# The gate projection's second half as one of SSD's concurrent streams

## The chip, the cores and the metric

The kernel runs on one core of one Trainium2 chip. The metric is the time of one execution in device microseconds (us). Before the change the median of three runs is 3372.4 us (3372.23 to 3380.13). The engines are TensorE (PE in rows; PEld its weight loads), VectorE (DVE), ScalarE (ACT), GpSimd (POOL) and SyncE (SP), which here only issues DMAs. Each engine works through its own list in a fixed order.

## The reference

The model is two transformer-like blocks on 1024 tokens of width 1024. The change lies in the first block's token mixers: a gated delta rule (GDN, 4 heads of 128) and a Mamba-2 SSD (8 heads of 64), each in both directions, both gated by a projection z of the same normalised tokens, and joined by an output projection.

```python
proj = h @ w_in
q, k, v, z_g, a_g, b_g, z_s, x_s, B_s, C_s, dt_s = _split(proj, GDN_SPLITS + SSM_SPLITS)
...
o = o_f + _flip(o_b)
o = rmsnorm(o, gdn_norm_g) * jax.nn.silu(z_g.reshape(Bsz, L, GDN_HEADS, GDN_DV).astype(f32))
...
y = y_f + _flip(y_b) + ssm_D.astype(f32)[:, None] * xs.astype(f32)
y = rmsnorm(y.reshape(Bsz, L, SSM_W) * jax.nn.silu(z_s.astype(f32)), ssm_norm_g)
mix = jnp.concatenate([o, y.astype(f32)], axis=-1).astype(h.dtype)
```

Only z_g (512 columns) and z_s (512 columns), their silu, and what multiplies them matter here. The output projection then multiplies mix by w_out, and the rest of the model follows.

## The kernel before

The kernel is written with a tile framework. Its program is emitted in an order of phases (phase_a, phase_gdn, phase_ssd, phase_mix, then the feed-forward part and the second block), and a list scheduler makes from it, ahead of time, one fixed list of instructions per engine; what is emitted earlier has priority, and a ready instruction of a later phase may be placed into a gap. Tiles come from pools with a number of buffers, so an instruction that takes a buffer waits for the last reader of the one it replaces.

phase_a projects the tokens and writes what later phases need to DRAM: the normalised tokens hxd (8 chunks of 128 tokens, each with a high and a low part, 1 MB a chunk), x (xtd), C (CTd), B (btd, BTd), k and v (ktd, vtd). Float32 products of the large projections are made of three matmuls in a reduced form, high by high, high by low, low by high.

phase_gdn works on 10 chunks (two of context) in two directions: a preparation (prep) for each of 20 chunk and direction pairs builds and inverts a triangular system on TensorE, VectorE and ScalarE in turns (Z products L580, D from a broadcast load, L496, in three buffers), and a step per pair carries the state and adds its output into oacc (L668). At its end the function zunits (L710) emits the gate projection zz: four quarters of 256 columns, each of which reads all 8 token chunks again (32 loads hx of 1 MB, L719, issued by GpSimd), 24 matmuls of 128x256 for a chunk (L722, 768 in all), a silu on 128x512 for two chunks (L725) and a write of the block to DRAM (zd, L726). It has one PSUM bank (psZ). It is emitted behind GDN, so the scheduler places it in gaps of GDN and among SSD.

phase_ssd (L728) drives several generators in turns: two chains of steps (L806 xe, L810 po, L826 pst), two of diagonal parts (diag: D0 and D1 masks and exps, xs, pcb, py L788), gdn_out (squares of oacc, L851, then the normalised and gated GDN output, L863) and ssd_out (product of yacc and the gate, L879, square L881, scaling L886, then chunk(): transposes ptm L909 and copies into the tile mixt). Each step and each diag loads its x, C and B from DRAM. mixt shares two on-chip slots (hx 2 and 3) with the gate's weights and tokens, so it waits for the last zz. phase_mix (L955) begins with the output projection pw (L980).

Of the kernel before, what the change touches and what calls it, by code (L numbers as in the profile page):

```python
# [23 lines left out]
def layout(inp):  # L24
    f = {k: np.asarray(v) for k, v in inp.items()}
    o = {}
# [25 lines left out]
    o["wz"] = np.ascontiguousarray(np.concatenate([zg, zs], 1).reshape(8, 128, 4, 256).transpose(2, 1, 0, 3))  # L52
# [68 lines left out]
class K:  # L121
# [63 lines left out]
    def phase_a(self):  # L185
# [136 lines left out]
        self.gcol = pp.tile([128, 1], F32, name="gcol")  # L322
        nc.gpsimd.dma_start(self.gcol, bass.AP(tensor=T["hp"].tensor, offset=T["hp"].offset + 56, ap=[[1, 128], [1, 1]]))
# [180 lines left out]
    def phase_gdn(self):  # L504
# [5 lines left out]
        psz = self.pool("psZ", 1, PSUM, ctx=zx)  # L510
# [21 lines left out]
        def prep(c, d, sl):  # L532
# [7 lines left out]
            D = ld.tile([128, 4, 128], F32, name="D")  # L540
# [76 lines left out]
        def step(c, d):  # L617
# [84 lines left out]
        self.zunits(psz, zp)  # L702
# [3 lines left out]
    def zunits(self, psz, zp):  # L706
        nc, T = self.nc, self.T
        HX = self.hx(3, [128, 2, 2, 8, 128], F32R)
        WZ = self.hx(2, [128, 2, 8, 256], F32R)
        for q in range(4):  # L710
            for k in range(0, 8, 2):
                raw = zp.tile([128, 2, 256], F32, name="raw")
                nc.sync.dma_start(raw, T["wz"][q][:, k:k + 2, :])
                self.split(WZ[:, 0, k:k + 2, :], WZ[:, 1, k:k + 2, :], raw)
            for c0 in range(0, 8, 2):
                zz = psz.tile([128, 2, 256], F32, name="zz")
                for i in range(2):
                    hx = HX[:, i]
                    nc.gpsimd.dma_start(hx, self.hxd[c0 + i])  # L719
                    for k in range(8):  # L720
                        for j, (a, b) in enumerate(((0, 0), (0, 1), (1, 0))):
                            nc.tensor.matmul(zz[:, i, :], hx[:, a, k, :], WZ[:, b, k, :],  # L722
                                             start=k == 0 and j == 0, stop=k == 7 and j == 2)
                zs = zp.tile([128, 2, 256], F32, name="zs")
                nc.scalar.activation(zs, zz, AF.Silu)  # L725
                nc.scalar.dma_start(self.zd[c0:c0 + 2, :, 256 * q:256 * q + 256].rearrange("c p f -> p c f"), zs)  # L726

    def phase_ssd(self):  # L728
# [7 lines left out]
        self.mixt = [[self.hx(i, [128, 8, 512], F32R) for i in (2, 3)]]  # L736
        self.psx = ExitStack()
# [11 lines left out]
        def loads(c, tag):  # L749
            x = ld.tile([128, 8, 64], F32, name="xt", tag="xt" + tag)  # L750
            nc.sync.dma_start(x.rearrange("p h f -> p (h f)"), self.xtd[c])
            ct = None
            if c < 8:
                ct = ld.tile([128, 2, 128], F32, name="CT", tag="CT" + tag)
                nc.sync.dma_start(ct, self.CTd[:, :, c * 128:(c + 1) * 128].rearrange("g p t -> p g t"))
            return x, ct

        def diag(c):
            x, ct = loads(c, "d")
            BT = ld.tile([128, 2, 128], F32, name="BT")  # L760
            nc.sync.dma_start(BT, self.BTd[:, :, c * 128:(c + 1) * 128].rearrange("g p t -> p g t"))
            xd = pr.tile([128, 8, 64], F32, name="xd")
            nc.gpsimd.tensor_tensor(xd, x, self.hp[:, 48:56, None].to_broadcast([128, 8, 64]), op=ALU.mult)
            D, X = [], []
# [78 lines left out]
        def gdn_out():  # L843
            ss = fp.tile([128, 8, 4], F32, name="ss")
            rs = fp.tile([128, 8, 4], F32, name="rs")
            for _ in range(6):
                yield
            for c in range(8):
                for h in range(4):
                    sq = fp.tile([128, 128], F32, name="sq", bufs=2)  # L850
                    nc.scalar.activation(sq, self.oacc[:, c, h, :], AF.Square, accum_out=ss[:, c, h:h + 1])  # L851
                yield
# [15 lines left out]
        def ssd_out():  # L868
            for i in range(4):
# [3 lines left out]
                while min(done[c] for c in cs) < 3:  # L873
                    yield
# [1349 lines left out]
```

## Time and profile before

| | us |
|---|---|
| median of three runs | 3372.4 |
| profiled execution | 3373.24 |
| its span in the trace | 3371.1 |
| TensorE busy in the span | 3088.8 |
| VectorE | 1841.7 |
| ScalarE | 1171.6 |
| GpSimd | 509.0 |

All times of the trace are from the start of the span. A stretch's busy time is what the engine's instructions fill. The granted clock is TensorE's, as a share of 2.4 GHz. An idle stretch of an engine counts only where the others wait for it. The rows that the prediction rests on stand below, each in a group with its view.

### The profile page before, as it was taken

What the parts mean: (1) busy time and instruction counts of PE and PEld (TensorE: products, weight loads), DVE (VectorE), ACT (ScalarE), POOL (GpSimd) and SP (SyncE); (2) the same over time, 40 slices, a digit from 0 to 9 for tenths busy, and PEclk for the clock granted to TensorE, in tenths of its full rate; (3) what the DMA queues carried; (4) which work ended last, traced back from release to release, by engine and by line L of the source; (5) the groups of instructions that cost most, each with busy time, mean ns of one, the idle gap of its engine ahead of it and who ended that gap; (6) DMA issues with size and microseconds to landing.
All of it is one profiled execution on the core that took longest, in us unless ns stands there. A gap on an engine that the chain in (4) does not pass through costs nothing. (4 is left out here: it accounts for less than half of the span.)

```text
span 3371.1 us, 43138 instructions
## 1 busy us (share of the span) xinstructions
PE 3088.8 (92%) x16679; PEld 2327.3 (69%) x16679; DVE 1841.7 (55%) x3344; ACT 1171.6 (35%) x2568; POOL 509.0 (15%) x416
## 2 busy tenths in 40 slices
PE   7999799877999999999999899999999997988886
PEld 3788689776788888888787787777777784322222
DVE  5754589557666564564778822458886454100000
ACT  4432455544432221122445512237775221111110
POOL 0000355344300000000233200000000101111110
PEclk9999799988999999999999999999999997999999
DMA  6942432786211111111211122200004458999996
GB/s 223 292 133 67 143 127 92 234 288 234 81 58 57 47 50 48 44 50 50 75 51 42 40 75 94 70 32 25 26 14 148 171 189 341 399 399 392 400 396 259
DMA packets 178188, 502.12 MB, mean 149 GB/s; under 512 B 21391, under 2 KB 85519, under 8 KB 148287
## 3 DMA queue, kind: packets, MB, share of 16 engines
q1 hardware_dynamic: 134928, 413.88, 33.5%
q0 software_dynamic: 14832, 52.81, 5.0%
q10 hardware_dynamic: 28223, 32.67, 2.7%
q8 instruction: 132, 2.16, 0.3%
q14 instruction: 73, 0.60, 0.1%
HBM read 450.39 MB, written 67.23 MB: 154 GB/s over the span
## 5 line engine op out<-in xcount | busy, mean ns | idle before, releaser
L2071 PE MATMUL ph<-wraw,xTt 128*64 128x512 f32 x1056 | 283.5, 606 | 49.1 <-DMA wraw<-in_w_dram 45.6
L158 ACT CAST wh<-wf 128x1024 fp32r<-128x1024 f32 x128 | 134.1, 1049 | 531.8 <-PE pg L943 187.2
L941 PE MATMUL pg<-hx,wh 128*128 128x512 f32 (+1 forms) x864 | 263.5, 385 | 8.5 <-DVE xt L1289 6.4
L943 PE MATMUL pg<-hx,wh 128*128 128x512 f32 (+1 forms) x864 | 262.4, 384 | 0.0
L945 PE MATMUL pg<-hx,wl 128*128 128x512 f32 (+1 forms) x864 | 262.1, 384 | 0.0
L2071 PEld LDWEIGHTS ph<-wraw,xTt 128*64 128x64 f32 x1056 | 84.5, 138 | 222.1 <-issue 122.6
L1069 DVE SCALAR_TENSOR_TENSOR acc<-pad,fcw,acc 128x1024 f32<-128x1024 f32 x176 | 226.0, 1284 | 21.3 <-ACT acc L1066 16.8
L159 DVE TENSOR_TENSOR wl<-wf,wh 128x1024 fp32r<-128x1024 f32 x96 | 117.0, 1219 | 136.2 <-ACT wh L158 135.6
L941 PEld LDWEIGHTS pg<-hx,wh 128*128 128x128 f32 x864 | 161.7, 190 | 41.5 <-ACT ainh L158 6.8
L943 PEld LDWEIGHTS pg<-hx,wh 128*128 128x128 f32 x864 | 161.7, 190 | 32.0
L945 PEld LDWEIGHTS pg<-hx,wl 128*128 128x128 f32 x864 | 161.5, 190 | 32.1 <-DVE wl L159 0.3
L722 PE MATMUL zz<-hx 128*128 128x256 f32 x768 | 131.7, 314 | 37.7 <-DMA hx<-hxd 21.0
L2088 PE MATMUL py<-wraw,hT 128*64 128x512 f32 x528 | 150.2, 601 | 3.7 <-issue 2.8
L2074 DVE SCALAR_TENSOR_TENSOR hs<-ph,gate,hs 128x256 f32<-128x256 f32 x32 | 15.5, 484 | 250.7 <-ACT hs L2073 250.7
L722 PEld LDWEIGHTS zz<-hx 128*128 128x128 f32 x768 | 109.2, 207 | 44.4 <-DMA hx<-hxd 15.4
L1027 POOL TENSOR_TENSOR sx<-sx,sqx 128x1024 f32<-128x1024 f32 x7 | 20.2, 2880 | 723.8 <-ACT sqx L1026 723.8
L1105 DVE SCALAR_TENSOR_TENSOR x<-pd,mod,x 128x1024 f32<-128x1024 f32 x42 | 53.9, 1282 | 136.3 <-PE pd L1100 136.3
L2092 DVE COPY yt<-py 128x512 f32<-128x512 f32 x33 | 22.8, 692 | 187.2 <-ACT yt L2091 187.2
L2073 ACT ACTIVATE hs<-ph 128x256 f32<-128x256 f32 x33 | 12.6, 383 | 282.0 <-PE ph L2071 282.0
L159 POOL TENSOR_TENSOR wl<-wf,wh 128x1024 fp32r<-128x1024 f32 x32 | 84.1, 2631 | 138.9 <-ACT wh L158 138.9
L225 PE MATMUL pj<-hxh,wh 128*128 128x512 f32 x320 | 103.4, 400 | 0.0
L225 PE MATMUL pj<-hxl,wh 128*128 128x512 f32 x320 | 102.6, 399 | 0.0
(702 smaller groups left out, 7565.6 us busy)
## 6 DMA issues: line engine op xcount, KB each, us to landing
wraw<-in_w_dram SPq DMA_DIRECT2D x132, 1024.0 KB, 22.3
wraw<-in_w2e_dram SPq DMA_DIRECT2D x66, 1024.0 KB, 22.9
hx<-hxd POOLq DMA_DIRECT2D x32, 1024.0 KB, 7.0
wa<-in_wadaT_dram SPq DMA_DIRECT2D x32, 512.0 KB, 5.0
wf<-in_wgate_dram SPq DMA_DIRECT2D x22, 512.0 KB, 3.2
wf<-in_wup_dram SPq DMA_DIRECT2D x22, 512.0 KB, 3.2
wf<-in_wconv_dram SPq DMA_DIRECT2D x20, 512.0 KB, 3.2
wdf<-in_wdown_dram SPq DMA_DIRECT2D x40, 256.0 KB, 2.6
```

Of the source, the lines that this page charges most:

```text
L158: nc.scalar.copy(hi, x)
L159: (eng or nc.vector).tensor_tensor(lo, x, hi.bitcast(F32), op=ALU.subtract)
L225: nc.tensor.matmul(ps[:, o:o + n], w[:, k, :], (hl if lo else hh)[:, k, ho:ho + n], start=k == 0 and i == 0, stop=k == 7 and i == 2)
L722: nc.tensor.matmul(zz[:, i, :], hx[:, a, k, :], WZ[:, b, k, :], start=k == 0 and j == 0, stop=k == 7 and j == 2)
L941: nc.tensor.matmul(ps[:, o:o + n], wh[:, k, :], xh[:, k, o:o + n], start=k == 0, stop=False)
L943: nc.tensor.matmul(ps[:, o:o + n], wh[:, k, :], xl[:, k, o:o + n], start=False, stop=False)
L945: self.lastmm = nc.tensor.matmul(ps[:, o:o + n], wl[:, k, :], xh[:, k, o:o + n], start=False, stop=k == nk - 1)
L1069: nc.vector.scalar_tensor_tensor(acc, pad[:, dy:dy + 16, dx:dx + 64], cw[:, f, tp:tp + 1], acc, op0=ALU.mult, op1=ALU.add)
L1105: nc.vector.scalar_tensor_tensor(x, pp, self.mod2[:, 24 + m:25 + m], x, op0=ALU.mult, op1=ALU.add)
L2071: nc.tensor.matmul(ph[m], x[:, k, m], f[s][:, j, :], start=k == 0, stop=k == 7)
L2088: nc.tensor.matmul(py[m, o * 512:o * 512 + 512], h[:, j, m], f[s][:, 2 * j + o, :], start=j == 0, stop=j == 1)
L2092: nc.vector.tensor_copy(y[:, 512:1024], py[:, 512:1024])
```

## The change

The weights are laid out as two halves of 512 columns, GDN's gate and SSD's gate. The function zunits goes away. The first half is emitted at the end of phase_gdn: all its weights are split once into two slots (hx 2, 3) from 16 raw loads of 128x256 through one buffer; tokens come in pieces of 256 KB (two of the eight 128-row blocks, high and low) into one tile hxs with room for two pieces, 4 loads a chunk, 32 in all; 24 matmuls of 128x512 a chunk; the silu is done in two halves of 256 columns through one buffer zs, each followed by a write.

The second half is a generator zgen in SSD's drive: four weight loads of 512 KB, split into the same two slots; per chunk (in the order 3, 4, 2, 5, 1, 6, 0, 7) two token loads of 512 KB into buffers that the output projection's weights also use (wpW), 24 matmuls, one silu, one write. ssd_out waits for zgen's chunk, and mixt is taken only when zgen is done. psZ's one bank stays through SSD, and SSD's own PSUM banks go from 6 to 5. In SSD x (10 tiles), C (one 1 MB load) and B by rows (one load) are loaded once and kept on chip; BT keeps a load per chunk. In GDN D has two buffers instead of three, and the squares of oacc move from gdn_out into the step that finishes a chunk.

```diff
-    o["wz"] = np.ascontiguousarray(np.concatenate([zg, zs], 1).reshape(8, 128, 4, 256).transpose(2, 1, 0, 3))
+    o["wz"] = np.ascontiguousarray(np.concatenate([zg, zs], 1).reshape(8, 128, 2, 512).transpose(2, 1, 0, 3))
...
-            D = ld.tile([128, 4, 128], F32, name="D")
+            D = ld.tile([128, 4, 128], F32, name="D", bufs=2)
...
+            nc.vector.tensor_add(oc, t, po2)
+            if c in seen:
+                for h in range(4):
+                    nc.scalar.activation(t[:, h, :], oc[:, h, :], AF.Square, accum_out=self.ssg[:, c, h:h + 1])
             seen.add(c)
-            nc.vector.tensor_add(oc, t, po2)
...
-        self.zunits(psz, zp)
+        self.zw = [self.hx(i, [128, 8, 512], F32R) for i in (2, 3)]
+        for k in range(16):
+            raw = zp.tile([128, 256], F32, name="raw")
+            f = (slice(None), k // 2, slice(256 * (k % 2), 256 * (k % 2) + 256))
+            nc.sync.dma_start(raw, T["wz"][0][f])
+            self.split(self.zw[0][f], self.zw[1][f], raw)
+        hx = zp.tile([128, 2, 4, 128], F32R, name="hxs")
+        for c in range(8):
+            zz = psz.tile([128, 512], F32, name="zz")
+            for k in range(0, 8, 2):
+                nc.gpsimd.dma_start(hx[:, :, k % 4:k % 4 + 2, :], self.hxd[c, :, :, k:k + 2, :])
+                for k2 in (k, k + 1):
+                    self.zmm(zz, hx[:, 0, k2 % 4, :], hx[:, 1, k2 % 4, :], k2)
+            for o in (0, 256):
+                zs = zp.tile([128, 256], F32, name="zs")
+                nc.scalar.activation(zs, zz[:, o:o + 256], AF.Silu)
+                nc.scalar.dma_start(self.zd[c, :, o:o + 256], zs)
         st.close()
         zx.close()
 
-    def zunits(self, psz, zp):
-        nc, T = self.nc, self.T
-        HX = self.hx(3, [128, 2, 2, 8, 128], F32R)
-        WZ = self.hx(2, [128, 2, 8, 256], F32R)
-        for q in range(4):
-            for k in range(0, 8, 2):
-                raw = zp.tile([128, 2, 256], F32, name="raw")
-                nc.sync.dma_start(raw, T["wz"][q][:, k:k + 2, :])
-                self.split(WZ[:, 0, k:k + 2, :], WZ[:, 1, k:k + 2, :], raw)
-            for c0 in range(0, 8, 2):
-                zz = psz.tile([128, 2, 256], F32, name="zz")
-                for i in range(2):
-                    hx = HX[:, i]
-                    nc.gpsimd.dma_start(hx, self.hxd[c0 + i])
-                    for k in range(8):
-                        for j, (a, b) in enumerate(((0, 0), (0, 1), (1, 0))):
-                            nc.tensor.matmul(zz[:, i, :], hx[:, a, k, :], WZ[:, b, k, :],
-                                             start=k == 0 and j == 0, stop=k == 7 and j == 2)
-                zs = zp.tile([128, 2, 256], F32, name="zs")
-                nc.scalar.activation(zs, zz, AF.Silu)
-                nc.scalar.dma_start(self.zd[c0:c0 + 2, :, 256 * q:256 * q + 256].rearrange("c p f -> p c f"), zs)
+    def zmm(self, zz, h, l, k):
+        for j, (a, b) in enumerate(((h, 0), (h, 1), (l, 0))):
+            self.nc.tensor.matmul(zz, a, self.zw[b][:, k, :], start=k == 0 and j == 0, stop=k == 7 and j == 2)
...
-        ps = self.pool("psS", 6, PSUM, ctx=st)
+        ps = self.pool("psS", 5, PSUM, ctx=st)
         pr = self.pool("sprep", 3, ctx=st)
-        ld = self.pool("sld", 3, ctx=st)
+        ld = self.pool("sld", 1, ctx=st)
...
+        X = [ld.tile([128, 8, 64], F32, name=f"X{c}") for c in range(10)]
+        CT = ld.tile([128, 2, 1024], F32, name="CT")
+        bts = ld.tile([128, 10, 256], F32, name="bts")
+
+        def load(c):
+            nc.sync.dma_start(X[c].rearrange("p h f -> p (h f)"), self.xtd[c])
+
+        for c in (8, 9):
+            load(c)
+        nc.sync.dma_start(bts, self.btd.rearrange("c p f -> p c f"))
+        nc.sync.dma_start(CT, self.CTd.rearrange("g p t -> p g t"))
+        for c in (0, 1, 7, 2, 6, 3, 5, 4):
+            load(c)
...
-                while min(done[c] for c in cs) < 3:
+                while min(done[c] for c in cs) < 3 or not zc.issuperset(cs):
...
-                    while gdone[0] < 2 * i + 2:
+                    while gdone[0] < 2 * i + 2 or not zdone:
                         yield
                     yield
+                    if not self.mixt:
+                        self.mixt.append([self.hx(i, [128, 8, 512], F32R) for i in (2, 3)])
                     for c in cs:
                         self.chunk(c)
                         yield
 
-        self.drive([chain(0), chain(1), diags(0), diags(1), gdn_out(), ssd_out()])
+        zc, zdone = set(), []
+
+        def zgen():
+            for k in range(0, 8, 2):
+                raw = self.wpW.tile([128, 8, 128], F32, name="wf").rearrange("p (a b) c -> p a (b c)", a=2)
+                nc.sync.dma_start(raw, T["wz"][1][:, k:k + 2, :])
+                self.split(self.zw[0][:, k:k + 2, :], self.zw[1][:, k:k + 2, :], raw)
+            yield
+            for c in (3, 4, 2, 5, 1, 6, 0, 7):
+                zz = self.psz.tile([128, 512], F32, name="zz")
+                hl = [self.wpW.tile([128, 8, 128], F32R, name=n) for n in ("wh", "wl")]
+                for j in range(2):
+                    nc.gpsimd.dma_start(hl[j], self.hxd[c, :, j])
+                for k in range(8):
+                    self.zmm(zz, hl[0][:, k, :], hl[1][:, k, :], k)
+                    if k % 4 == 3:
+                        yield
+                zs = fp.tile([128, 512], F32, name="zs")
+                nc.scalar.activation(zs, zz, AF.Silu)
+                nc.scalar.dma_start(self.zd[c, :, 512:1024], zs)
+                zc.add(c)
+            zdone.append(1)
+
+        self.drive([chain(0), chain(1), diags(0), diags(1), zgen(), gdn_out(), ssd_out()])
```

The lists of the engines before and after are the same from the first pw matmul on. Ahead of it these places differ.

TensorE, from the last po of GDN (from vo and P) into SSD's first matmuls, before (zz is the gate projection, pcb, pst, po and py are SSD's):

```order
4862 L663 MATMUL po_7273<-vo,P 128x128 x4
4863 L722 MATMUL zz<-hx 128x256 x37
4864 L775 MATMUL pcb<-CT,BT 128x128 x2
4865 L722 MATMUL zz<-hx 128x256 x48
4866 L775 MATMUL pcb<-CT,BT 128x128 x2
4867 L826 MATMUL pst<-xe,bt 128x256 x4
4868 L722 MATMUL zz<-hx 128x256 x48
4869 L826 MATMUL pst<-xe,bt 128x256
4870 L722 MATMUL zz<-hx 128x256 x24
4871 L826 MATMUL pst<-xe,bt 128x256 x3
4872 L810 MATMUL po<-hT_8250,CT 128x256
4873 L722 MATMUL zz<-hx 128x256 x6
```

The same place after:

```order
4793 L729 MATMUL zz<-hx,hxs 128x512
4794 L665 MATMUL po_7302<-vo,P 128x128 x4
4795 L729 MATMUL zz<-hx,hxs 128x512 x26
4796 L785 MATMUL pcb<-CT,BT 128x128 x4
4797 L835 MATMUL pst<-xe,bts 128x256
4798 L729 MATMUL zz<-hx,hxs 128x512 x12
4799 L835 MATMUL pst<-xe,bts 128x256 x4
4800 L729 MATMUL zz<-hx,hxs 128x512 x6
4801 L835 MATMUL pst<-xe,bts 128x256
4802 L729 MATMUL zz<-hx,hxs 128x512 x6
4803 L835 MATMUL pst<-xe,bts 128x256 x2
4804 L819 MATMUL po<-hT_7697,CT 128x256 x2
```

Before, 217 of 768 zz stand ahead of GDN's last solve (pn) and 264 ahead of the first pcb; after, 19 and 50 of 384.

TensorE, from SSD's last matmuls to the first pw, before:

```order
5057 L788 MATMUL py<-xs_8941,D_8934 128x64
5058 L826 MATMUL pst<-xe,bt 128x256 x4
5059 L810 MATMUL po<-hT_8250,CT 128x256 x2
5060 L810 MATMUL po<-hT_8251,CT 128x256 x2
5061 L909 MATMUL ptm<-cst,hx 128x128 x32
5062 L980 MATMUL pw<-hx,wh 128x512 x3
5063 L980 MATMUL pw<-hx,wl 128x512
```

After (the zz from wh and wl tiles are zgen's; what is left out between the pieces is zz alone, with two ptm):

```order
4980 L798 MATMUL py<-xs_8448,D_8441 128x64
4981 L819 MATMUL po<-hT_7698,CT 128x256 x2
4982 L729 MATMUL zz<-hx,wh 128x512 x2
4983 L729 MATMUL zz<-hx,wl 128x512
...
5061 L729 MATMUL zz<-hx,wl 128x512
5062 L938 MATMUL ptm<-cst,hx 128x128 x6
5063 L729 MATMUL zz<-hx,wh 128x512 x2
...
5111 L729 MATMUL zz<-hx,wl 128x512
5112 L938 MATMUL ptm<-cst,hx 128x128 x24
5113 L1009 MATMUL pw<-hx,wh 128x512 x3
5114 L1009 MATMUL pw<-hx,wl 128x512
```

All 192 zz of zgen stand behind SSD's last po, and 8 of the 32 transposes ptm stand between them; before there is no zz behind SSD's last zz groups, and the 32 ptm follow po at once.

ScalarE, at the end of SSD's exps (L502 in before, L503 after), before:

```order
480 L725 ACT_TABLE_LOAD
481 L725 ACTIVATE zs<-zz 128x512
482 L502 ACT_TABLE_LOAD
483 L502 ACTIVATE D_8891<-D_8891,fneg 128x128
484 L726 DMA zd<-zs 128x2x256
485 L881 ACTIVATE sqy,sy<-hx 128x512
486 L502 ACTIVATE D_8934<-D_8934,fneg 128x128 x8
487 L725 ACT_TABLE_LOAD
488 L725 ACTIVATE zs<-zz 128x512
489 L881 ACTIVATE sqy,sy<-hx 128x512
490 L726 DMA zd<-zs 128x2x256
```

After (zs of L722 are the two halves of a block, CAST of wf is zgen's weights):

```order
487 L722 ACT_TABLE_LOAD
488 L722 ACTIVATE zs<-zz 128x256
489 L503 ACT_TABLE_LOAD
490 L503 ACTIVATE D_8441<-D_8441,fneg 128x128
491 L723 DMA zd<-zs 128x256
492 L503 ACTIVATE D_8441<-D_8441,fneg 128x128 x2
493 L722 ACT_TABLE_LOAD
494 L722 ACTIVATE zs<-zz 128x256
495 L723 DMA zd<-zs 128x256
496 L722 ACTIVATE zs<-zz 128x256
497 L723 DMA zd<-zs 128x256
498 L158 CAST hx<-wf 128x1024 x4
499 L919 ACTIVATE zs<-zz 128x512
```

Each block of a chunk now has two silus with a write between them, and exps and their table load stand between the halves; the casts of zgen's weights stand behind the last half. In all 27 table loads stand in SSD's part of the list, 18 before.

## Rows read from the trace of the kernel before

**Rows 1.** Head of the page.
```profile
span 3371.1 us, 43138 instructions
```

**Rows 2.** Timeline, TensorE and VectorE: start us, us, engine, line, operation, count [idle].
```profile
628.71 0.69 DVE L668 TENSOR_TENSOR hx<-ot,po 128x512 f32<-128x512 f32 x1 [4.26 <-POOL ot L666]
...
804.87 2.08 PE L810 MATMUL po<-hT,CT 128*128 128x256 f32 x8 [2.21 <-DVE hT L832]
...
829.40 1.94 PE L909 MATMUL ptm<-cst,hx 128*128 128x128 f32 x8 [4.02 <-DVE hx L886]
...
832.66 1.20 PE L980 MATMUL pw<-hx,wh 128*128 128x512 f32 x2
```

**Rows 3.** Stretches: length, busy us (instructions) by engine, clock, DMA share, GB/s.
```profile
400.00:628.00 228.00, 216.06 (x2937) 207.33 (x2934) 193.22 (x506) 125.30 (x368) 110.09 (x125) 0.98 0.34 109
...
640.00:800.00 160.00, 129.66 (x881) 120.56 (x880) 82.95 (x107) 79.18 (x191) 74.51 (x74) 0.91 0.85 283
...
820.00:840.00 20.00, 12.97 (x45) 9.61 (x44) 18.03 (x63) 4.57 (x8) 0.00 (x0) 0.54 0.80 288
```

**Rows 4.** Waits, 640 to 840: who waited for what, us, times, longest.
```profile
POOL hx L719 <- PE zz L722: 46.2, 11, 9.1
...
PE zz L722 <- DMA hx<-hxd: 17.8, 7, 4.3
...
ACT L725 <- DMA zd<-zs: 13.9, 4, 4.7
...
PE ptm L909 <- DVE hx L863: 11.3, 1, 11.3
```

**Rows 5.** Timeline, TensorE: the gate projection, and 512-column matmuls of the output projection.
```profile
790.22 3.13 PE L722 MATMUL zz<-hx 128*128 128x256 f32 x24
...
863.98 0.39 PE L980 MATMUL pw<-hx,wl 128*128 128x512 f32 x1
864.21 0.62 PE L980 MATMUL pw<-hx,wh 128*128 128x512 f32 x2
```

**Rows 6.** Stretches: zz (L722) alone, then VectorE's Z products (L580) alone.
```profile
400.00:420.00 20.00, 1.45 (x6) 0.90 (x6) 0.83 0.17 48
460.00:480.00 20.00, 7.45 (x35) 5.10 (x35) 0.93 0.42 144
...
400.00:420.00 20.00, 7.16 (x17) 0.83 0.17 48
460.00:480.00 20.00, 6.70 (x16) 0.93 0.42 144
```

**Rows 7.** Timeline, GpSimd: the start of GDN.
```profile
377.15 1.04 POOL L538 TENSOR_TENSOR kt<-kt,erest 128x512 f32<-128x512 f32 x1 [4.82 <-DMA kt<-ktd]
```

**Rows 8.** Groups by line, 628.7 to 833: busy us, mean ns, idle before.
```profile
L851 ACT ACTIVATE sq<-hx 128x128 f32<-128x128 f32 x32 | 9.4, 297 | 0.4 <-DVE hx L668 0.4
```

**Rows 9.** Timeline, TensorE: SSD's matmuls py (fp32, 64 columns) and pst (256 columns).
```profile
684.08 3.10 PE L788 MATMUL py<-xs,D 128*128 128x64 f32 x24
...
800.71 1.95 PE L826 MATMUL pst<-xe,bt 128*128 128x256 f32 x8
```

**Rows 10.** Timeline, ScalarE: a silu, its write, and an exp behind its table load.
```profile
640.50 0.60 ACT L725 ACTIVATE zs<-zz 128x512 f32<-128x512 f32 x1 [4.11 <-PE zz L722]
...
641.53 1.28 ACT L502 ACT_TABLE_LOAD   x1
642.82 0.99 ACT L502 ACTIVATE D<-D,fneg 128x128 f32<-128x128 f32 x3
```

**Rows 11.** DMA, 640 to 840: total, then issues: count, KB, median us to landing.
```profile
DMA packets 26356, 54.59 MB, mean 273 GB/s; under 512 B 2375, under 2 KB 14663, under 8 KB 23908
...
hx<-hxd POOLq DMA_DIRECT2D x19, 1024.0 KB, 8.1
...
zy<-zd SPq DMA_DIRECT2D x8, 256.0 KB, 2.9
...
raw<-in_wz_dram SPq DMA_DIRECT2D x7, 256.0 KB, 4.4
```

More of the change, by code (lines that the diff above doesn't have):

```diff
@@ L322, in phase_a @@
         self.gcol = pp.tile([128, 1], F32, name="gcol")
+        self.ssg = pp.tile([128, 8, 4], F32, name="ssg")
         nc.gpsimd.dma_start(self.gcol, bass.AP(tensor=T["hp"].tensor, offset=T["hp"].offset + 56, ap=[[1, 128], [1, 1]]))
@@ L509, in phase_gdn @@
         zp = self.pool("zs", 1, ctx=zx, side="right")
-        psz = self.pool("psZ", 1, PSUM, ctx=zx)
+        self.psx = ExitStack()
+        psz = self.psz = self.pool("psZ", 1, PSUM, ctx=self.psx)
         self.oacc = self.hx(0, [128, 8, 4, 128])
@@ L735, in phase_ssd @@
         self.yacc = self.hx(1, [128, 8, 8, 64])
-        self.mixt = [[self.hx(i, [128, 8, 512], F32R) for i in (2, 3)]]
-        self.psx = ExitStack()
+        self.mixt = []
         self.psm = self.pool("psM2", 2, PSUM, ctx=self.psx)
-        ps = self.pool("psS", 6, PSUM, ctx=st)
+        ps = self.pool("psS", 5, PSUM, ctx=st)
         pr = self.pool("sprep", 3, ctx=st)
-        ld = self.pool("sld", 3, ctx=st)
+        ld = self.pool("sld", 1, ctx=st)
         hp = self.pool("shp", 1, ctx=st)
@@ L747, in bank, with cut @@
             return ps.tile(shape, F32, name=name, tag="b")
[L749 to L756, printed above, removed]
+        X = [ld.tile([128, 8, 64], F32, name=f"X{c}") for c in range(10)]
[9 more added lines that the diff above has]
+            load(c)
+        def cut(t, c):
+            return t[:, :, 128 * c:128 * c + 128]
         def diag(c):
[L759 to L762, printed above, removed]
+            x, ct = X[c], cut(CT, c)
+            bT = ld.tile([128, 2, 128], F32, name="BT", bufs=3)
+            nc.sync.dma_start(bT, self.BTd[:, :, c * 128:(c + 1) * 128].rearrange("g p t -> p g t"))
+            xd = pr.tile([128, 8, 64], F32, name="xd", bufs=2)
             nc.gpsimd.tensor_tensor(xd, x, self.hp[:, 48:56, None].to_broadcast([128, 8, 64]), op=ALU.mult)
-            D, X = [], []
+            D, xw = [], []
             for d in range(2):
@@ L771, in diag @@
                 nc.vector.tensor_tensor(xs, x, self.sp[:, c, 12 * d + 4:12 * d + 12, None].to_broadcast([128, 8, 64]), op=ALU.mult)
-                X.append(xs)
+                xw.append(xs)
             pc = bank("pcb", [128, 2, 128])
             for g in range(2):
-                nc.tensor.matmul(pc[:, g, :], BT[:, g, :], ct[:, g, :], start=True, stop=True)
+                nc.tensor.matmul(pc[:, g, :], bT[:, g, :], ct[:, g, :], start=True, stop=True)
             yield
@@ L787, in diag @@
                 for d in range(2):
-                    nc.tensor.matmul(py[:, h, :], D[d][:, h, :], X[d][:, h, :], start=d == 0, stop=d == 1)
+                    nc.tensor.matmul(py[:, h, :], D[d][:, h, :], xw[d][:, h, :], start=d == 0, stop=d == 1)
             oc = self.yacc[:, c]
@@ L799, in step @@
         def step(c, d):
-            x, ct = loads(c, f"s{d}")
-            bt = ld.tile([128, 2, 128], F32, name="bt", tag=f"bt{d}")
-            nc.sync.dma_start(bt.rearrange("p g f -> p (g f)"), self.btd[c])
+            x, ct = X[c], cut(CT, c) if c < 8 else None
+            bt = bts[:, c, :].rearrange("p (g f) -> p g f", g=2)
             last = c == (7 if d == 0 else 0)
@@ L843, in gdn_out @@
         def gdn_out():
-            ss = fp.tile([128, 8, 4], F32, name="ss")
+            ss = self.ssg
             rs = fp.tile([128, 8, 4], F32, name="rs")
[L846 to L851, printed above, removed]
+            for _ in range(14):
                 yield
```

## The prediction

> **What bounds the kernel now.** I read the page's head first: the span is 3371.1 us [rows 1]; the profiled execution took 3373.2 us, 2.1 more than the span and 0.8 more than the median of the runs shown (3372.4), so a change of the span is added to 3373.2. The two orders read alike, on every engine, from the first matmul of the output projection (pw) on. So the whole effect is how much earlier or later the first pw starts. In before it starts at 832.66 us; the last GDN instruction on VectorE starts at 628.71 and SSD's last po run at 804.87 [rows 2]. The stretch to look at is therefore GDN, then 204.0 us from GDN's end to pw.
>
> Then the table of stretches [rows 3]. From 400 to 628 VectorE is busy 193.2 of 228 us, TensorE 216.1, but TensorE's list there is full of the gate projection (zz), which fills its pauses. From 640 to 800 no engine is full (TensorE 129.7 of 160) and the DMA share is 0.85: token loads, 1 MB each, and SSD's own reads share the DMA engines. The list of waits names them: zz waits for hx loads, the loads' issue on GpSimd waits for zz, ScalarE waits for the write of a gate block, and the tail waits for VectorE's output gating [rows 4]. From 820 to 840 the granted clock is 0.54 and TensorE is busy 13.0 of 20 us, VectorE 18.0: the tail is VectorE's.
>
> **GDN (term 1).** Before places 240 of the 768 zz (256 columns) ahead of GDN's end; after places 24 of 384 (512 columns). At full clock 24 zz of 256 columns take 3.13 us with the last one's own drain, so 0.12 each; of 512 columns, a second matmul adds 0.62 − 0.39 = 0.23 [rows 5]. So TensorE is freed of 240 × 0.12 − 24 × 0.23 = 23.3 us. What is that worth? Compare two equal windows: with 6 zz VectorE did 17 Z products, with 35 zz it did 16 [rows 6]. So 29 zz, 3.5 us of TensorE, cost one Z of seventeen, 20/17 = 1.2 us, a third at most, and the first window ran at the lower clock. I take −6 us (bounds 0 and −23.3). At GDN's start GpSimd waits 4.82 us for a kt load [rows 7] while 1 MB token loads are moving; the new loads there are two of 256 KB: −4 (0 to −4.8). The 32 squares, 9.4 us of ScalarE [rows 8], come into GDN, each four behind a sum of VectorE; ScalarE has room (125.3 of 228 us [rows 3]), but its next casts feed VectorE: +1.5 (0 to +9.4). D with two buffers: 0, hidden by a preparation's length; if one landing of 4.4 us in four of the 20 showed, +22. Term 1 is −8.5.
>
> **SSD with the first half (term 2).** TensorE's own work falls. Before, 528 zz × 0.12 = 63 us lie behind GDN's end. SSD's matmuls are unchanged: 256 py at 0.12 (24 in 3.10 us with the last one's drain), 64 po and 72 pst at (1.95 − 0.39)/7 = 0.22 [rows 9], 32 pcb at py's interval, about 64 us. After, 168 zz × 0.23 = 38 us are left of the first half until SSD's last po; the floor is 38 + 64 = 102 us where before needed 178 (628.7 to 806.7).
>
> But the first half is now a ring with little room: one PSUM bank, one gate buffer, and a token tile filled in pieces, two pieces ahead. After a chunk's last zz, ScalarE loads the silu table (1.28 us), does half a block (at most 0.60), and the second half waits until the first has been written out; then table load and silu again [rows 10]. The nearest landing is the 256 KB raw load of this stretch, 4.4 us [rows 11] (before's wait for the gate write is up to 4.7 at a time [rows 4]). That is 1.28 + 0.60 + 4.4 + 1.28 + 0.60 = 8.2. Meanwhile the next chunk's first two pieces have landed. Then six zz (1.4), the third piece's issue and landing (4.4), its six (1.4), the fourth's six (1.4): 8.6. To these 16.8 I add 0.9 per chunk for standing behind SSD's instructions in TensorE's and GpSimd's fixed order (an estimate). Seven chunks are left at GDN's end: 7 × 17.7 = 124 us. The bounds are the floor of 102 and, with the landing of a 1 MB load (8.1 [rows 11]) at both places, 7 × 25.1 = 176.
>
> Here ScalarE pays 27 table loads (14 silu, 13 exp) in place of 18. In the trace a load takes 1.28 us and the exp behind it starts 0.01 us after its end [rows 10]. The Trainium skill (ScalarE: Activation LUTs, What ACT_TABLE_LOAD costs) puts a drain of about 1.38 us on top, 2.66 us for a switch; by it the ring would be 2.8 us longer, 20.5, and seven of them would turn −11 into +8, no change. The trace shows no such pause, so the sum keeps 1.28.
>
> **The second half, zgen (term 3).** All of its 192 zz stand behind SSD's last po. From the last zz of the first half: table load, half silu, landing, half silu are 6.9 us, then ScalarE's cast of the first weights, 1024 columns where the silu of 512 takes 0.60, so about 1.2, and VectorE's subtraction, put at the same: 9.3. Chunk one, with weights arriving, 6; then seven times 24 × 0.23 = 5.5 plus 1.2 for the silu that frees the only bank and the restart: 46.9. The token loads are prefetched (8.1 us for twice the size, and 6.7 us per chunk are there). In the middle TensorE's six transposes ptm wait for VectorE's gated GDN output; before such a wait took 11.3 us [rows 4]; it has half of zgen's time ahead of it, so 5 (0 to 11.3). Sum 67 (bounds 44, the bare matmuls, and 117, eight unhidden landings of 8.1).
>
> **To pw (term 4).** The last chunk's product with its gate stands in VectorE's list ahead of the last copies for pw, so pw waits for the write (4.4), the read back (2.9 [rows 11]) and then what before took from the transposes behind the last gating to pw, 832.66 − 829.40 = 3.3 [rows 2]: 10.5. The bound below is 3.3, above 19 with 8.1 twice.
>
> **Sum.** 124 + 67 + 10.5 = 201.5 against 204.0, so −2.5, and −8.5 in GDN: −11. Forecast 3373.2 − 11 = 3362 us. SSD gets 54 us shorter (178 to 124) and 26 us of old tail (204 − 178) lie beside zgen; of these 80 us the serial second half and its tail take 77.5 back.
>
> **Rivals.** *A, the floor is reached.* With DMA freed (54.59 MB moved from 640 to 840 [rows 11]; of the 32 MB of token loads 16 go, and x, C and B are read once) pieces land in about 3 us and lie hidden behind SSD's matmuls, so that SSD runs near TensorE's 102 us plus 13 of start, zgen in 55, the tail in 8: 178 − 204 = −26. With zz in GDN worth half of the 23.3, GDN gives −11.7 − 4 + 1.5 = −14: −40, 3333 us. For it: no engine is full, and before's waits on hx are 17.8 us. Against it: one bank and in-order issue remain.
>
> *B, slower: cover lost.* In before zz sat under GDN's VectorE work at nearly no price [rows 6] and its loads there had time. After, every zz of chunk 1 to 7 needs two landings in the ring with GpSimd's issues queued behind xe, masks and sums. The price is 14 exposed landings, so each us by which one exceeds 4.4 costs 14 us. The point from which it decides: at 5.2 us the gain is gone, at 5.9 the kernel is slower by over 0.3%, at 6.9 (bound: the 1 MB's 8.1) it ends at 3362 + 35 = 3397. For it: a DMA share of 0.85 in before, and 4.4 is the median only of its own kind. The Trainium skill (DMA: Bandwidth & Descriptors, Bandwidth) speaks against the small pieces: batch transfers to at least 1 MiB, a 1 MB load taking 6.15 us there. In rows: one 1 MB at 8.1 against four of 4.4, 17.6 one after another, 9.5 more a chunk; only if the pieces run one by one, which two slots ahead prevent in part. By that rule in full the seven chunks cost 66 us more than whole loads would; I hold that to be a part of B.
>
> *C, no change.* GDN is not shortened by the absence of zz, since VectorE sets its pace (term 1 at −1 instead of −8.5): 3370. That the change does not do what it says can be excluded: the order shows zz, loads and buffers moved.
>
> **Chances.** About 0.3% (10 us) is what a measurement of this kernel can tell from no change. Forecast 0.42, of which 0.30 faster and 0.12 within; A 0.16, faster; C 0.17, of which 0.14 within and 0.03 slower; B 0.25, of which 0.02 within. Faster 0.46, same 0.28, slower 0.26. The forecast's own range is 3348 to 3376. To hold 8 in 10, it reaches to the middle of A and most of B: 3332 to 3394.
>
> **What would show it.** GDN's last sum on VectorE near 620; the start of zz chunks in SSD about 17.7 us apart, with ScalarE's second silu waiting for a DMA; SSD's last po near 744; zgen's zz in one run of 65 to 70 us with a pause before six transposes; pw near 822, behind a wait for zy. A shows in chunks 13 us apart and po before 735; B in chunks over 19 us and GpSimd's token issues waiting. The forecast is wrong if zz chunks run beside SSD without pauses, or if VectorE's gating comes so late that the tail after zgen is over 20 us.

## The result

The changed kernel takes 3397.6 us (median of four runs; a fifth took 4411.9 us at a granted clock of 0.65 and is left out), 25 us more than the 3372.4 of before; the ratio is 1.0068 (95% interval 1.0049 to 1.0087), about 23 us. The forecast of 3362 and its range, 3332 to 3394, were missed. Rival B had the time, 3397, but not by the price that it named.

The span and the places that the forecast named, in the changed kernel's page and timeline (start, length, engine, line, operation, count, idle before):

```profile
span 3399.6 us, 42324 instructions
...
623.41 0.69 DVE L669 TENSOR_TENSOR hx<-ot,po 128x512 f32<-128x512 f32 x1 [4.12 <-POOL ot L668]
...
764.81 1.08 PE L819 MATMUL po<-hT,CT 128*128 128x256 f32 x4
777.61 0.79 PE L729 MATMUL zz<-hx,wh 128*128 128x512 f32 x1 [11.72 <-ACT hx L158]
...
850.83 0.39 PE L729 MATMUL zz<-hx,wl 128*128 128x512 f32 x1
...
863.61 1.65 PE L1009 MATMUL pw<-hx,wh 128*128 128x512 f32 x3
```

Against [rows 2]: GDN ends 5.3 us earlier, pw starts 30.9 us later, and the span is 28.5 longer (2.4 come back behind pw; where was not followed).

| stretch | before | forecast | after |
|---|---|---|---|
| GDN's end | 628.7 | 620.2 | 623.4 |
| to SSD's last po | 178 | 124 | 142.1 |
| zgen, to its last zz | in SSD | 67 | 85.7 |
| to pw | 26 | 10.5 | 12.4 |

Stretches of the changed kernel for its zz alone (start and end, length, TensorE busy and count, weight loads, clock, DMA share, GB/s): GDN's preparations, SSD, zgen.

```profile
407.80:612.40 204.60, 6.74 (x15) 2.85 (x15) 0.94 0.21 62
623.40:766.00 142.60, 53.12 (x168) 36.07 (x168) 0.89 0.53 164
766.00:851.00 85.00, 58.44 (x192) 42.75 (x192) 0.80 0.72 248
```

Fifteen zz lie beside GDN's preparations, and the clock is 0.80 in zgen. The DMA share in SSD fell from 0.85 [rows 3] to 0.53: DMA was freed, and SSD still was slow.

**SSD.** Each chunk's first zz in the changed kernel's timeline:

```profile
646.82 3.08 PE L729 MATMUL zz<-hx,hxs 128*128 128x512 f32 x12 [1.65 <-ACT zs L722]
...
666.68 3.00 PE L729 MATMUL zz<-hx,hxs 128*128 128x512 f32 x12
...
687.49 3.01 PE L729 MATMUL zz<-hx,hxs 128*128 128x512 f32 x12
...
709.28 3.12 PE L729 MATMUL zz<-hx,hxs 128*128 128x512 f32 x12
...
734.22 3.12 PE L729 MATMUL zz<-hx,hxs 128*128 128x512 f32 x12
...
755.93 2.98 PE L729 MATMUL zz<-hx,hxs 128*128 128x512 f32 x12
```

They are 19.9, 20.8, 21.8, 24.9 and 21.7 us apart, where 17.7 was forecast. It is not longer landings. DMA issues from 640 to 770 (count, KB, median us to landing), then who waited from 640 to 765 (us in all, times, longest):

```profile
hxs<-hxd POOLq DMA_DIRECT2D x24, 256.0 KB, 3.3
...
zd<-zs ACTq DMA_DIRECT2D x14, 128.0 KB, 1.8
wf<-in_wz_dram SPq DMA_DIRECT2D x2, 512.0 KB, 10.2
```

```profile
ACT zs L722 <- PE zz L729: 34.0, 5, 11.3
POOL hxs L717 <- PE zz L729: 26.2, 15, 4.8
ACT D L503 <- POOL D L498: 19.8, 6, 7.3
...
PE zz L729 <- DMA hxs<-hxd: 12.9, 5, 4.6
```

Pieces land in 3.3 us and gate writes in 1.8, both under the 4.4 assumed. (Only from 612 to 647, where SSD's own loads start, are the medians over it: 5.2 for five pieces, 5.1 for four writes.) With these landings and a half silu of 0.38 us the ring would be 5.1 + 7.5 = 12.6 us. ScalarE stands 34 us at a silu whose zz are not done, with SSD's exps behind it in its list; GpSimd stands 26 us at token issues, with the masks behind. Both wait for TensorE.

What TensorE did meanwhile is read from the five chunks that begin between 646.8 and 734.2: all engines (columns as in [rows 3]), then zz alone, then the second silu that freed the bank for the zz at 666.68.

```profile
646.80:755.90 109.10, 94.01 (x508) 79.13 (x509) 71.37 (x95) 69.59 (x154) 71.74 (x68) 0.94 0.45 131
...
646.80:755.90 109.10, 36.40 (x120) 24.66 (x121) 3.84 (x10) 0.94 0.45 131
...
661.24 0.38 ACT L722 ACTIVATE zs<-zz 128x256 f32<-128x256 f32 x1
```

TensorE is busy 94.0 of the 109.1 us: 36.4 with zz, 57.6 with SSD's own matmuls. That is 7.3 and 11.5 us a chunk; the 3.0 left are mostly waits for token pieces (12.9 us in five waits), which are issued only when the zz of an earlier piece are done. The five chunks from 666.68 on begin without any idle time before them. The bank had been free for 3.2 to 5.9 us by then (5.1 at 666.68), and TensorE was working through SSD's matmuls that stand there in its list. So from 646.8 on it is not the ring of bank, silu and write that sets the pace, but the list of TensorE, with SSD's matmuls between the zz. This is read from the trace; no run moves that list alone.

**zgen.** From the last po, TensorE pauses 11.7 us for the first weights; from the last zz of the first half, where the forecast began its 9.3, it is 13.5. The first chunk takes until 793.4, 15.8 us instead of 6, and seven take 57.8 instead of 51.9. SyncE's, TensorE's and GpSimd's rows there:

```profile
766.71 1.30 SPq L991 DMA_DIRECT2D x<-in_xT_dram  x3
768.06 1.19 SPq L906 DMA_DIRECT2D wf<-in_wz_dram  x2
```

```profile
779.89 1.06 PE L729 MATMUL zz<-hx,wh 128*128 128x512 f32 x2
...
781.17 1.06 PE L729 MATMUL zz<-hx,wh 128*128 128x512 f32 x2
...
786.43 0.49 PE L729 MATMUL zz<-hx,wh 128*128 128x512 f32 x1 [2.60 <-ACT hx L158]
...
798.05 0.63 PE L729 MATMUL zz<-hx,wh 128*128 128x512 f32 x2
...
798.74 0.63 PE L729 MATMUL zz<-hx,wh 128*128 128x512 f32 x2
...
810.14 0.70 PE L729 MATMUL zz<-hx,wh 128*128 128x512 f32 x2 [2.77 <-DMA wh<-hxd]
```

```profile
802.37 1.29 POOL L883 TENSOR_TENSOR hx<-hx,zy 128x512 f32<-128x512 f32 x1 [8.69 <-DMA zy<-zd]
```

The weights are issued behind x loads of the next phase, and land in 10.2 us among them. The zz behind the pause run at half clock, 1.2 GHz: two take 1.06 us against 0.63, and the granted clock is 0.59 from 777.6 to 797.3 and 1.00 from 797.3 to 807. Three zz take 1.28 us there (779.89 to 781.17) and 0.69 later (798.05 to 798.74), so the 24 zz of the first chunk lose some 4.7 us by it (an estimate from these rows); its pauses for weights come to 3.8 (0.47, 2.60 and 0.77). At 810 a token load is late, issued at 803.6 behind a product that had waited 8.69 us for zy. The ptm in zgen's middle waited for nothing, where 5 us had been put.

### The profile page after: what moved, and what is told of

It reads as the page before. It is cut to its first block, busy times and chain, and to the rows that moved or that the text cites. A ratio compares the mean times of both kernels' runs of the same rounds, so it can differ in the third digit from the quotient of the medians.

```text
span 3399.6 us, 42324 instructions
## 1 busy us (share of the span) xinstructions
PE 3108.4 (91%) x16295; PEld 2314.2 (68%) x16295; DVE 1836.5 (54%) x3348; ACT 1177.7 (35%) x2582; POOL 525.6 (15%) x432
## 5 line engine op out<-in xcount | busy, mean ns | idle before, releaser
L1098 DVE SCALAR_TENSOR_TENSOR acc<-pad,fcw,acc 128x1024 f32<-128x1024 f32 x176 | 226.0, 1284 | 21.3 <-ACT acc L1095 16.8
L159 DVE TENSOR_TENSOR wl<-wf,wh 128x1024 fp32r<-128x1024 f32 x96 | 117.0, 1219 | 131.8 <-ACT wh L158 131.0
L159 POOL TENSOR_TENSOR wl<-wf,wh 128x1024 fp32r<-128x1024 f32 x32 | 84.1, 2630 | 131.4 <-ACT wh L158 131.4
L225 PE MATMUL pj<-hxh,wl 128*128 128x512 f32 x320 | 100.6, 395 | 0.0
L158 ACT CAST wdh<-wdf 128x512 fp32r<-128x512 f32 (+1 forms) x44 | 25.5, 583 | 201.9 <-PE pd L1129 190.2
## 6 DMA issues: line engine op xcount, KB each, us to landing
wst<-in_wada_dram SPq DMA_DIRECT2D x16, 512.0 KB, 10.2
```

What stands on the lines that cost most here:

```text
L158: nc.scalar.copy(hi, x)
L159: (eng or nc.vector).tensor_tensor(lo, x, hi.bitcast(F32), op=ALU.subtract)
L225: nc.tensor.matmul(ps[:, o:o + n], w[:, k, :], (hl if lo else hh)[:, k, ho:ho + n], start=k == 0 and i == 0, stop=k == 7 and i == 2)
L1098: nc.vector.scalar_tensor_tensor(acc, pad[:, dy:dy + 16, dx:dx + 64], cw[:, f, tp:tp + 1], acc, op0=ALU.mult, op1=ALU.add)
```

## The experiments

Every time stands beside runs of the kernel before on the same chip, whose median was 3376.2 (e1 to e4), 3378.7 (e5 to e8), 3376.6 (e9, e10) and 3374.6 (e11).

**e1. Weight splits on GpSimd.** Why so few zz lay in GDN: the subtractions of the weight splits on VectorE, changed kernel, L159:

```profile
424.90 0.42 DVE L159 TENSOR_TENSOR hx<-raw,hx 128x256 fp32r<-128x256 f32 x1
...
459.54 0.72 DVE L159 TENSOR_TENSOR hx<-raw,hx 128x256 fp32r<-128x256 f32 x1
...
573.43 0.41 DVE L159 TENSOR_TENSOR hx<-raw,hx 128x256 fp32r<-128x256 f32 x1
```

Between the first and the last of these rows, 148 us apart, there is one; one raw buffer joins each load to the split before.

```diff
-            self.split(self.zw[0][f], self.zw[1][f], raw)
+            self.split(self.zw[0][f], self.zw[1][f], raw, nc.gpsimd)
```

> The changed kernel, but the low parts of the first half's weights are computed on GpSimd instead of VectorE. Theory 'starved weights': in the changed kernel the 16 splits stood in VectorE's list behind GDN's work (one between 120 and 220 us of GDN, so that only 24 of 192 zz of the first half lay in GDN); on GpSimd they are free early, some 109 zz go ahead of GDN's last solve, the first half is done when SSD's py begin, and the second half lies beside SSD. GDN's end stays near 624 to 630, SSD needs 155 to 165 us for 127 us of TensorE's work, the tail 20 to 25: first pw near 805, about 3345 us, 25 to 30 below before. Theory 'pieces' (the ring of 256 KB pieces, one PSUM bank and half silus costs 21 us a chunk wherever it stands): the same zz at the same 21 us a chunk, no gain on the changed kernel, 3395 to 3405.

Measured 3378.9, ratio 1.0006 (0.9995 to 1.0016): 22 us under the changed kernel's ratio, and no faster than before. Zz were 120 by GDN's end and all lay ahead of SSD's last po, but the preparations took 229 us and GDN ended at 655.6. Neither theory holds whole. The preparations are read from the line of R, one per preparation (count, ns of one, first and last start): before, changed, e1.

```profile
L606 DVE TENSOR_TENSOR R<-cst,pn x20: 679/681/690, 413.8 to 619.2; 128x512 f16<-128x512 f32 x20
```

```profile
L608 DVE TENSOR_TENSOR R<-cst,pn x20: 671/680/689, 407.8 to 612.4; 128x512 f16<-128x512 f32 x20
```

```profile
L608 DVE TENSOR_TENSOR R<-cst,pn x20: 670/680/687, 416.8 to 645.9; 128x512 f16<-128x512 f32 x20
```

205.4 us with 198 zz in between, 204.6 with 15, 229.1 with 100. The first two are 0.8 us apart, but profiles spread by more than that. The four other runs with 15 zz there (e2, e7, e8, e11) took 200.1 to 204.0, the two with 198 and 196 (e3, e4) 206.3 and 206.5. Zz alone in e2 and in e4:

```profile
412.00:612.10 200.10, 6.50 (x15) 2.60 (x15) 0.00 (x0) 0.97 0.21 64
```

```profile
415.00:621.50 206.50, 42.22 (x196) 28.65 (x196) 2.39 (x4) 1.00 0.36 110
```

So 183 more zz of 256 columns, 22 us of TensorE, cost the preparations 0.8 to 6.4 us, 3.7 between the means.

**e2. Two weight loads of zgen emitted at SSD's start.**

```diff
+        for k in range(2):
+            nc.sync.dma_start(zr[k], T["wz"][1][:, 2 * k:2 * k + 2, :])
...
```

> The changed kernel, but the first two of the four weight loads of the second half are issued at the start of SSD, ahead of the x loads of the later phase in SyncE's list. Theory 'queue': TensorE's pause of 11.7 us ahead of the second half and the one of 2.6 us in its first chunk come from these loads standing behind x loads that wait for SSD's buffers; the first falls to about 3 us and a part of the half clock behind it goes: 10 to 14 us less than the changed kernel, 3385 to 3390. Rival: the loads are only late because all transfers there share the DMA engines (0.87 to 0.99 busy from 766 to 788), token loads land no earlier, and the time stays within 4 us of 3399.

3402.0, ratio 1.0080 (1.0066 to 1.0094): no gain. The loads did not move: they were issued at 772.6, behind x again. Their buffers lie in the space of the first half's gate and token tiles, which comes free with its last silu. The queue theory was not tested by it.

**e3, e4. Parts alone in the kernel before.** e3 keeps x, C and B on chip; e4 has D in two buffers and the squares in the step.

```diff
-            x, ct = loads(c, "d")
+            x, ct = X[c], cut(CT, c)
...
```

> The kernel before with one edit of the change: x, C and B of SSD loaded once and kept on chip. Theory 'DMA shares': some 6 MB less among 54.6 MB, token loads land sooner, SSD ends 5 to 10 us earlier, 3363 to 3368. Rival: the waits are set by the ring of token buffers and the lists' order; within 3 us of before (3372).

```diff
-            D = ld.tile([128, 4, 128], F32, name="D")
+            D = ld.tile([128, 4, 128], F32, name="D", bufs=2)
...
```

> The kernel before with the two edits of GDN alone: D in two buffers, squares in the step. Theory: GDN is VectorE's, the squares take room on ScalarE that is there, D loads stay ahead: GDN's end at 629 to 632, the squares are gone from SSD's start, total within 3 us of 3372. Rival: four squares behind each sum hold up ScalarE's casts, GDN's end 5 to 9 us later, 3377 to 3381.

e3: 3375.6, ratio 0.9993 (0.9983 to 1.0002); e4: 3377.6, ratio 1.0004 (0.9991 to 1.0016). No difference for either: in e3 the rival held, in e4 the theory. Neither makes the loss. Nor does the PSUM bank that SSD gave up, by itself: e5 and e6 below do without it too, and are faster than before.

**e5. Weights split in place.**

```diff
-            raw = zp.tile([128, 256], F32, name="raw")
-            nc.sync.dma_start(raw, T["wz"][0][f])
+            lo = self.zw[1][:, k:k + 2, :]
+            nc.gpsimd.dma_start(lo, T["wz"][0][:, k:k + 2, :])
+            self.split(self.zw[0][:, k:k + 2, :], lo, lo.bitcast(F32))
```

> The changed kernel, but the first half's weights come by four loads of 512 KB on GpSimd's queue straight into the tile of their low parts, and are split there (cast to the high tile, subtraction in place), so that no raw buffer links one load to the split before it. The last run with splits on GpSimd made GDN 32 us longer; its preparations took 229 us against 204.6 without zz and 205.4 with 198 zz of 256 columns. Theory 'raw ring': there the zz stood in TensorE's list waiting for a raw load, cast and split in turn, and GDN's work behind them; without the ring 133 zz lie in GDN at next to nothing, as in before: preparations 205 to 212, GDN's end 624 to 632, all zz before SSD's end, first pw at 810 to 825, 3350 to 3365 us. Rival 'zz of 512 columns cost': a zz of 0.23 us delays GDN's chain wherever it stands, preparations 225 to 235, GDN's end 645 to 655, 3375 to 3385.

3368.2, ratio 0.9970 (0.9960 to 0.9981), about 33 us under the changed kernel by the ratios ((1.0068 − 0.9970) × 3372). Here 144 zz lie ahead of GDN's end and all 384 ahead of SSD's last po. GDN ends at 644.9, 21.5 us later than in the changed kernel, but the first pw comes at 829.4, so 55.7 us less are left behind GDN. Stretch of the preparations, zz alone, then two waits of e1 from 412 to 650:

```profile
420.30:635.20 214.90, 43.08 (x109) 19.28 (x109) 1.00 0.28 77
```

```profile
ACT hx L158 <- DMA raw<-in_wz_dram: 11.7, 4, 4.4
POOL hx L159 <- ACT hx L158: 10.4, 7, 4.3
```

With 109 zz of 512 columns, 25 us of TensorE, the preparations are 10 us longer than in the changed kernel and 15 longer than in e2: not 25 and not 0. They are 14 us shorter than in e1, where ScalarE waited 11.7 us for raw loads and GpSimd 10.4 for their casts. This edit takes out the raw ring and GpSimd's subtractions together, so what the ring alone cost in e1 is not shown.

**e6. In place for both halves, two gate buffers.**

```diff
-                zs = zp.tile([128, 256], F32, name="zs")
+                zs = zp.tile([128, 256], F32, name="zs", bufs=2)
...
```

> As the run with weights split in place, for both halves (the second half's four loads on GpSimd's queue too), and with two buffers for the half silus of the first half. Theory 'ring of the gate block': the second buffer takes the wait for the first write (1.8 to 4.7 us) and one pair of table loads per chunk out; with 7 chunks of which 5 lie in SSD, 8 to 15 us below the in-place run. Rival: the lists' order, not the buffer, holds the chunks back: within 4 us of the in-place run.

3360.0, ratio 0.9946 (0.9931 to 0.9960): faster than both kernels. First pw:

```profile
825.13 1.63 PE L1008 MATMUL pw<-hx,wh 128*128 128x512 f32 x3
```

It is 7.5 us before that of before [rows 2], though GDN ended at 643.5; behind GDN 181.6 us are left of 204. The difference to e5, some 8 us, holds two edits, so the gate buffer's share is not shown.

**e7. x loads emitted one by one with the output weights.**

```diff
...
+            if h == 0:
+                nc.sync.dma_start(x1[:, m, :], T["xT"][:, m, :])
```

> The changed kernel, but the eight x loads of the later phase are emitted one by one with the output projection's weights instead of all at its start. Theory 'shared landing': the first weights of the second half take 10 us because they come free with the x loads and the first tokens and share the DMA engines with them; alone they land in 4 to 5 us, TensorE's pause ahead of zgen falls from 11.7 to 6 to 7 us, 4 to 8 us below the changed kernel: 3391 to 3395. Rival: tokens (four loads of 512 KB) are enough to fill the engines, 3397 to 3402.

3401.8, ratio 1.0066 (1.0045 to 1.0086). The scheduler put three x loads ahead of the weights as before, so this tested nothing either.

**e8. One half silu per chunk.**

```diff
-            for o in (0, 256):
-                zs = zp.tile([128, 256], F32, name="zs")
-                nc.scalar.activation(zs, zz[:, o:o + 256], AF.Silu)
+            zs = zp.tile([128, 256], F32, name="zs")
+            nc.scalar.activation(zs, zz[:, 0:256], AF.Silu)
+            for o in (0, 256):
```

> The changed kernel with one half silu per chunk of the first half: the silu of columns 256 to 511 is left out, and the first 256 columns' block is written in both places, so no second silu waits for a write. The lists come out otherwise too: all zz stand ahead of SSD's last po. Theory 'ring': this wait and the order that the scheduler builds around it hold the first half back and with it the second; the first half is done by SSD's middle, SSD ends at 780 to 800, first pw at 810 to 830, 3355 to 3375. Rival: the half silus are beside SSD's work, and what counts is that too few zz lie in GDN: 3390 to 3400.

3381.9, ratio 1.0012 (1.0001 to 1.0022), 19 us under the changed kernel, above the 3375 expected. With 27 zz by GDN's end, nearly as few as there, all 384 lay ahead of SSD's last po (834.5 for 765.5). The 165 left of the first half took 101 us (625.7 to 726.7), 14.7 a chunk where the changed kernel needed 21.1. So the half silus, with the order of the lists that comes with them, cost some 19 us without any cover; how much of it is the silu and how much the order is not separated.

**e9. The kernel before without the cover.**

```diff
+                if q == 0 and k == 0:
+                    nc.vector.tensor_copy(raw[:, 0, 0:32], self.oacc[:, :, :, 0].rearrange("p c h -> p (c h)"))
```

> The kernel before with one wait added: the first weights of the gate projection wait for the last GDN sum (a copy of 32 columns of it into the raw tile, which the load then overwrites), so that none of the 240 zz that stood in GDN stand there. Theory 'cover': in GDN they were free (preparations 205.4 us with 198 zz, 204.6 with 15), behind it they cost. GDN's end moves to 620 to 624 through the earlier start alone, preparations stay at 203 to 206; behind it 768 zz need 92 us of TensorE and 32 MB of loads where 22 MB took 178 us of SSD: SSD's last po 25 to 40 us later, 3395 to 3415 us. Rival: SSD has room (TensorE 129.7 of 160 us busy), takes most of it, 3375 to 3385.

3438.6, ratio 1.0178 (1.0161 to 1.0195): worse than either theory. Zz alone, preparations and the two stretches behind GDN; then the first pw:

```profile
414.70:613.60 198.90, 0.00 (x0) 0.00 (x0) 0.96 0.19 57
623.00:796.00 173.00, 78.02 (x480) 70.05 (x480) 0.86 0.83 277
796.00:872.00 76.00, 47.24 (x288) 44.03 (x288) 0.78 0.73 252
```

```profile
901.90 1.51 PE L982 MATMUL pw<-hx,wh 128*128 128x512 f32 x3
```

```profile
  ACT hx L158: 36.4, 12
  DMA hx<-hxd: 36.0, 18
```

Preparations without zz take 198.9 us, 6.5 less than with 198. Pw is 69 us later: 240 zz that are 29 us of TensorE cost 0.29 us each behind GDN. The last two rows say what ended TensorE's idle time ahead of zz (us, times): casts of weights, and token loads. The 24 zz of one token load, 2.9 us of TensorE, take about 8 us behind GDN in both kernels: 32 loads from 623 to 872 here, 22 in 178 us before.

**e10. Weights of e6 behind GDN's first loads.**

```diff
+            nc.gpsimd.tensor_copy(lo[:, 0, 0:64], lvl[:, 0, 0, :])
...
```

> As the run with weights split in place and two gate buffers, but the four loads of the first half's weights wait for the table lvl that GDN loads at its start (a copy of 64 of its columns into each piece of the tile, which the load overwrites). There the first preparation ended at 424.0 us, 16 us later than in the changed kernel, since 2 MB of weights and GDN's first loads came at once. Theory 'start': the first preparation ends at 406 to 414, the rest keeps its pace, 8 to 14 us less than that run: 3346 to 3352. Rival: the first chunk's zz then miss the wide gaps, or TensorE waits for the weights in its list inside GDN, and the time stays at 3356 to 3364.

3360.8, ratio 0.9954 (0.9940 to 0.9967), as e6. The first R still came at 423.2 (424.0 in e6); the start theory fell. Ahead of it ran 36 zz, 33 in e6 and 4 in the changed kernel; whether they hold it back was not tested.

**e11. zgen's weights alone in place.**

```diff
-                raw = self.wpW.tile([128, 8, 128], F32, name="wf").rearrange("p (a b) c -> p a (b c)", a=2)
-                nc.sync.dma_start(raw, T["wz"][1][:, k:k + 2, :])
+                lo = self.zw[1][:, k:k + 2, :]
+                nc.gpsimd.dma_start(lo, T["wz"][1][:, k:k + 2, :])
```

> The changed kernel, but the second half's weights alone come by four loads on GpSimd's queue straight into the tile of their low parts, which is free when the first half's last zz has read it; the buffers that they had before lie in the space of the first half's gate and token tiles and came free only with its last silu, together with those of the x loads and the first tokens. Theory 'space': TensorE's pauses of 11.7 and 2.6 us at zgen's start fall to 7 to 9 together and less of its first chunk runs at half clock: 6 to 12 us below the changed kernel, 3388 to 3394. Rival: the tokens' buffers lie in the same space and land as late as the weights did, 3396 to 3402.

3395.7, ratio 1.0061 (1.0044 to 1.0078); the interval overlaps the changed kernel's. The first weights were cast at 762.0 instead of 776.5, but zgen started later:

```profile
782.19 1.22 PE L729 MATMUL zz<-hx,wh 128*128 128x512 f32 x2 [16.02 <-ACT zs L722]
```

The casts now stand ahead of the last half silus in ScalarE's list, and these free the bank. What the pause at zgen's start is worth is left open.

## Why the prediction was wrong

- *Reading the lists* was right: 24 zz by GDN's end, 192 by SSD's last po, a serial zgen, pw behind the last gate's product.
- *Term 1* came to −5.3 for −8.5: −6.0 by the first R (407.8 for 413.8), −0.8 by the preparations, +1.5 from the last R to GDN's end. One pair of profiles does not hold this split: in e2, e7, e8 and e11 the first R comes at 409.8 to 413.4, and the zz that left GDN are worth 0.8 to 6.4 us, 6.5 by e9. So the −6 put on the zz is within what was measured, and the −4 put on the start is not shown.
- *Term 2* is a step that failed, +18. "To these 16.8 I add 0.9 per chunk for standing behind SSD's instructions" lets SSD's matmuls run in the waits of a ring that sets the pace. In the trace 11.5 us of them a chunk lie between the zz in TensorE's list, with 7.3 of zz and 3.0 of waits: 21.8 for 17.7. The ring's parts were shorter than forecast (the landings taken as 4.4 were 3.3 and 1.8) and no longer decided from 646.8 on. The first chunk and the wait ahead of it took 23.4 (DMA share 1.05, clock 0.64), and the last chunk only 9.6 to the last po.
- *Term 3* failed by as much, +18.7. "Chunk one, with weights arriving, 6" was 15.8: half clock and late weights. The start took 13.5 for 9.3 from the last zz of the first half, and the seven other chunks 5.9 more than forecast. Its upper bound of 117 does not follow either: 44 of matmuls and eight landings of 8.1 are 109. *Term 4*, +1.9.
- *Rival B* named cover and the ring, and gave 3397. Its signs came (chunks over 19 us, GpSimd's token issues waiting), but its price did not: landings were over 4.4 us only at SSD's start, and 3.3 and 1.8 from 647 on. That its number fits is luck. Its first half, the lost cover, is what the runs bear out: e9 takes the cover from before and loses 69 us at pw; e5 gives the first half its place in GDN again and brings 33 us back. The weights' way kept it out, one raw buffer and VectorE's list: 24 zz by GDN's end, 120 with the subtractions on GpSimd (e1), 144 without the raw buffer (e5). The 33 us are not the cover alone, since in e5 the second half also lies beside SSD; e8 gets some 19 of them without cover. That the second half stood behind SSD follows from the weights' shared slots, in the lists; it was not tested by itself.
- *Rival A* had its condition, pieces in about 3 us, and still fell: TensorE was busy 115.8 of the 142.6 us from 623.4 to 766, not near 102; the zz took 53.1 where 38 had been put, at a granted clock of 0.89. *C* fell with the time.
- The drain that the Trainium skill (ScalarE: Activation LUTs, What ACT_TABLE_LOAD costs) puts on top of a table load, 2.66 us for a switch, shows in no row here. In the changed kernel a silu ends at 656.75 and the exp behind the switch starts at 658.06, 1.31 us later:

```profile
656.37 0.38 ACT L722 ACTIVATE zs<-zz 128x256 f32<-128x256 f32 x1
656.77 1.28 ACT L503 ACT_TABLE_LOAD   x1
...
658.06 1.86 ACT L503 ACTIVATE D<-D,fneg 128x128 f32<-128x128 f32 x6
```

## What to carry to other kernels

Count how much of a filler's work lies under a stage that another engine paces. There it is cheap (183 zz of 256 columns, 22 us of TensorE, for 0.8 to 6.4 us here; 94 more of 512 columns, as much of TensorE, for 10 to 15 in e5, which holds other edits too), and the same instructions behind the stage can cost more than their own time (0.29 us for 0.12). A filler of larger units needs all its inputs before the first unit; when those come through one buffer and the pacing engine, the filler misses the stage. Where two streams share one engine's fixed list, add the work of both: the waits of one hide the work of the other only where the list puts it there (11.5 us a chunk here, for the 0.9 that was added).

## What the runs showed of the hardware

Little beyond the times above. From 640 to 770, 128 KB gate writes land in 1.8 us (median of 14) and 256 KB pieces in 3.3 (of 24). Of eleven 512 KB loads issued from 766.7 to 771.6, the two of weights took 10.2 us and the four of tokens 9.9 and 11.1 (medians of the high and the low parts), the five of x 4.9. A change of the activation table took 1.31 us from the end of a silu to the start of an exp.
